# Attention's matmuls in a written order on TensorE, and every other instruction placed by the scheduler on its timeline model

## The chip, the cores and the metric

The kernel runs on one core of one Trainium2 chip. The metric is the device time of one execution in microseconds (us): the kernel before takes 2864.3 us (median of 3 runs, 2860.72 to 2870.65). The trace quoted below is of one further execution of the same kernel, which took 2866.75 us; its span, from the first to the last recorded instruction, is 2865.0 us.

## What is computed

One decoder layer for 2048 prompt tokens and 32 sample tokens (8 sequences of 4), model width 1024. Two branches read the same projection of the normed input: an HGRN2 recurrence (4 heads, a 128 by 128 state each) and sliding-window attention (window 128, 8 query heads on 2 key heads, a sink in the softmax). Gates merge them, and a squared-ReLU feed-forward network follows.

```python
h = _rmsnorm(x, n1)
z = h @ w_in                                   # hq, hf, hi, hg, sq, sk, sv, ga, gb
f = lb + (1.0 - lb) * jax.nn.sigmoid(hf)
o_hg, s_new = _hgrn_recurrence(heads(hq), heads(jnp.log(f)), heads(1.0 - f), heads(hi), s0, 64)
o_hg = _rmsnorm(o_hg, hg_norm_w)
y_a = (o_hg * jax.nn.silu(hg)) @ w_up_a
q, k = _rotary(sq, pos), _rotary(sk, pos)
o_b = _swa_prompt(q, k, v, sinks)              # or _swa_sample for the sample tokens
y_b = o_b @ w_up_b
x = x + (jax.nn.sigmoid(ga) * y_a + jax.nn.sigmoid(gb) * y_b) @ w_o
h2 = _rmsnorm(x, n2)
x = x + jnp.square(jax.nn.relu(h2 @ w_ff1)) @ w_ff2
```

## The kernel before, in words

Five engines work from queues of their own, each in order: PE (TensorE: matmuls, transposes), DVE (VectorE), ACT (ScalarE), POOL (GpSimd) and SP (DMA issues). Every large product is made in three matmuls, because each float32 operand is split into a high and a low part in the type fp32r: high by high, high by low, low by high. In the trace these are the three lines L162, L163, L164 (`gemm_T`), L188 to L190 (`gemm_NK`) or L262 to L264 (`prod`). Scores, transposes and the HGRN products work in plain float32, in matmuls of 128 columns.

The tokens stand in four blocks of 512, b0 to b3; b3 also carries the 32 sample tokens. Blocks b0 and b1 make the half "sb 0", b2 and b3 "sb 1". For sb 0 the in-projection is made block by block; for sb 1 a stage z makes most of it first by Strassen's scheme into memory (tiles fB_z, fC_z, fD_z are its PSUM sums, zS and zA its operands), and b2 and b3 load their parts back. Each block then runs through:

- the remaining projections (hi: tile ps_hib, 96 matmuls of 512 columns in four banks);
- `rotary_T`, which rotates a chunk's queries and keys on POOL (L896 to L899), transposes them on PE (qT, kT) and copies them out on ACT; then `swa_scores` and `swa_values` for the four chunks c0 to c3 of 128 tokens (sp: scores, pT: transposed probabilities, po: values). For b3 the attention of the sample tokens stands ahead of that (sps, pTs, po_s);
- the columns hf of the projection (ps_hfb, four times 24 matmuls), then the HGRN levels (`hgrn_levels`, tiles lv L747 and lx L781) with the columns hg between them;
- per head group the chain o, u, on, kn, oT (L1085 to L1132): PE sums o, ACT squares it, POOL raises it to a power (ors, L195 and L197), DVE scales (on, L1092), PE transposes; u updates the state. For b3 the sample tokens' recurrence follows (o_smp and us, L1141 to L1163), for which SP loads one state per head (L1149);
- the gates b and a (tiles gbb, ybb, gab, yab) and the output projection wob.

After both halves the feed-forward stages f0 and f1 (Strassen again, tiles fB_f, fC_f, fD_f) and f2 (tile f) run. In the Strassen stages seven products share a few PSUM banks; the running sum of a bank is copied out by ACT (L325) or DVE (L327) before the next product adds to it ("snapshot"), and that matmul waits for the copy. `ff_sums` (L578) makes the operand sums of the first feed-forward half: SP loads h2 (L587), four DVE operations sum (L598 to L601), POOL's queue issues the four stores of dS (L603). This is placed beside block 2.

PSUM has the rings mm, tp, hg and sw of two banks each, handed out in program order. What runs when on each engine is decided by the tile framework's scheduler, by priorities that follow the program's order. Only places where the program itself interleaves (a hook between weight groups, hg columns at the rounds 2, 3, 4 and 6 of the levels) are set by hand.

## Time and profile before

| | before |
|---|---|
| three timed runs, us | 2870.65, 2860.72, 2864.3 |
| the profiled execution, us | 2866.75 |
| its span, us | 2865.0 |
| PE busy, us | 2776.3 (97% of the span) |
| DVE, ACT, POOL busy, us | 1786.9, 1113.8, 493.9 |
| mean granted clock of PE | 0.992 |
| instructions in the trace | 50058 |

An engine's busy time counts the time in which at least one of its instructions ran. PE's busy time is no measure of its pace, since matmuls overlap and a matmul at half the clock is busy twice as long; so three things are read for PE: where it idles and for whom, at which clock it runs (a column of the table by stretches), and how far apart the starts of its matmuls lie.

### The profile page before, as it was taken

The page shows a single profiled execution, that of the slowest core. Times are in us where ns is not written, and L with a number is a line of the kernel's source. Part 1 is how long each engine was busy: PE and PEld are TensorE (multiplying, and loading weights), DVE is VectorE, ACT ScalarE, POOL GpSimd, SP SyncE. Part 2 cuts the span into 40 slices and gives each one's busy share as a digit, 9 for nine tenths or more (in the row PEclk, how much of TensorE's full clock was granted, in tenths as well). Part 3 has the DMA queues.
Part 4 walks back from the last instruction along what each step waited for, and adds up shares of the span by engine and source line. Part 5 has one row for each costly group of instructions (what it writes and reads, how often), then busy time and mean ns, then how long its engine had stood idle before and what let it go on. Part 6 is the DMA issues. An engine that isn't in the chain of part 4 may idle for free.

```text
span 2865.0 us, 50058 instructions
## 1 busy us (share of the span) xinstructions
PE 2776.3 (97%) x20053; PEld 2421.9 (85%) x20053; DVE 1786.9 (62%) x2889; ACT 1113.8 (39%) x2070; POOL 493.9 (17%) x782
## 2 busy tenths in 40 slices
PE   8999999999999998999999999999998999999998
PEld 7778877788799966777888888877888999999998
DVE  5585755745765367535766777766567776664546
ACT  4542344423444343234424333434343333343342
POOL 1100211102310112330122221120003343320001
PEclk9999999999999999999999999999999999999999
DMA  5237662277743425642346544697556444485553
GB/s 189 62 91 250 199 200 59 79 252 245 242 142 98 153 61 185 203 139 84 99 154 203 172 155 140 222 318 251 191 192 219 151 145 156 139 294 180 186 186 123
DMA packets 344481, 487.60 MB, mean 170 GB/s; under 512 B 23432, under 2 KB 220824, under 8 KB 344248
## 3 DMA queue, kind: packets, MB, share of 16 engines
q1 hardware_dynamic: 289112, 329.10, 36.5%
q0 software_dynamic: 42880, 140.22, 13.4%
q10 hardware_dynamic: 12256, 15.08, 1.5%
q8 instruction: 157, 2.57, 0.4%
q14 instruction: 76, 0.62, 0.1%
HBM read 353.64 MB, written 130.68 MB: 169 GB/s over the span
## 4 chain that ended last, share of the span: by engine, by line
PE 78%; DMA 7%; issue 5%; DVE 5%; ACT 2%; POOL 2%; SPq 0%; POOLq 0%; ACTq 0%; DVEq 0%
PE f L1494 6%; PE f L1493 6%; PE f L1495 6%; PE fB_f L262 4%; PE fB_f L264 4%; PE fB_f L263 4%; PE fD_f L262 2%; PE fD_f L264 2%; PE fD_f L263 2%; PE fB_z L262 1%; PE fB_z L264 1%; PE fB_z L263 1%; PE wob L1302 1%; PE wob L1303 1%; PE wob L1301 1%
## 5 line engine op out<-in xcount | busy, mean ns | idle before, releaser
L1493 PE MATMUL f<-f2S,hw2T 128*128 128x264 f32 (+1 forms) x576 | 184.3, 320 | 2.8 <-ACT hw2T L148 2.8
L1495 PE MATMUL f<-f2S,lw2T 128*128 128x264 f32 (+1 forms) x576 | 184.3, 320 | 1.1 <-DVE lw2T L149 1.1
L1494 PE MATMUL f<-f2S,hw2T 128*128 128x264 f32 (+1 forms) x576 | 184.0, 319 | 0.0
L262 PE MATMUL fB_f<-S,w1T_f 128*128 128x264 f32 (+1 forms) x384 | 123.0, 321 | 3.2 <-ACT c_f L325 2.2
L1493 PE MATMUL f<-f2A,h_w2B 128*128 128x264 f32 (+1 forms) x384 | 122.4, 319 | 0.0
L1494 PE MATMUL f<-f2A,h_w2B 128*128 128x264 f32 (+1 forms) x384 | 122.3, 318 | 0.0
L1495 PE MATMUL f<-f2A,l_w2B 128*128 128x264 f32 (+1 forms) x384 | 122.3, 318 | 0.0
L263 PE MATMUL fB_f<-S,w1T_f 128*128 128x264 f32 (+1 forms) x384 | 122.3, 319 | 0.0
L264 PE MATMUL fB_f<-S,w1T_f 128*128 128x264 f32 (+1 forms) x384 | 121.9, 319 | 0.0
L149 DVE TENSOR_TENSOR lw2T<-lw2T,hw2T 128x1024 fp32r<-128x1024 f32 x64 | 78.2, 1223 | 69.3 <-ACT hw2T L148 68.6
L148 ACT CAST hw2T<-lw2T 128x1024 fp32r<-128x1024 f32 x64 | 67.2, 1050 | 134.5 <-DMA lw2T<-w_T 134.5
L1493 PEld LDWEIGHTS f<-f2S,hw2T 128*128 128x128 f32 x576 | 108.8, 189 | 11.2 <-ACT hw2T L148 3.7
L1495 PEld LDWEIGHTS f<-f2S,lw2T 128*128 128x128 f32 x576 | 108.4, 188 | 9.5 <-DVE lw2T L149 1.9
L1494 PEld LDWEIGHTS f<-f2S,hw2T 128*128 128x128 f32 x576 | 108.7, 189 | 7.5
L1303 PE MATMUL wob<-m_b,l_wob 128*128 128x512 f32 (+2 forms) x320 | 112.0, 350 | 2.8 <-DVE l_wob L255 2.8
L1301 PE MATMUL wob<-m_b,h_wob 128*128 128x512 f32 (+2 forms) x320 | 112.2, 351 | 0.5 <-ACT m_b L254 0.5
L1302 PE MATMUL wob<-m_b,h_wob 128*128 128x512 f32 (+2 forms) x320 | 112.1, 350 | 0.3 <-DVE m_b L255 0.2
L149 DVE TENSOR_TENSOR f2S<-f2S 128x1024 fp32r<-128x1024 f32 (+1 forms) x64 | 79.1, 1240 | 43.8 <-ACT f2S L148 43.4
L254 ACT CAST w1T_f<-w1r_f 128x512 fp32r<-128x512 f32 x128 | 77.3, 620 | 71.4 <-DVE w1r_f L298 32.4
L255 DVE TENSOR_TENSOR w1T_f<-w1r_f,w1T_f 128x512 fp32r<-128x512 f32 x128 | 87.1, 687 | 27.0 <-ACT w1T_f L254 26.7
L1420 POOL DMA_DIRECT2D u_A<-c_f x106 | 57.5, 543 | 235.3 <-DVE c_f L1404 223.7
L1420 POOL DMA_DIRECT2D u_S<-s_f x144 | 77.9, 542 | 110.9 <-DVE s_f L1415 89.3
(839 smaller groups left out, 9375.7 us busy)
## 6 DMA issues: line engine op xcount, KB each, us to landing
w1r_f<-w_ff SPq DMA_DIRECT2D x64, 512.0 KB
lw2T<-w_T SPq DMA_DIRECT2D x64, 512.0 KB
rw2B<-w_ff SPq DMA_DIRECT2D x48, 512.0 KB
f2S<-u_S SPq DMA_DIRECT2D x32, 528.0 KB
ws<-w_ff SPq DMA_DIRECT2D x32, 512.0 KB
r_wob<-w_o SPq DMA_DIRECT2D x32, 512.0 KB
f2S<-u_S SPq DMA_DIRECT2D x32, 512.0 KB
u_S<-s_f POOLq DMA_DIRECT2D x96, 132.0 KB, 2.2
```

The source lines that it names most:

```text
L149: nc.vector.tensor_tensor(lo, F(lo), F(hi), ALU.subtract)
L255: nc.vector.tensor_tensor(dl, src, F(dh), ALU.subtract)
L262: nc.tensor.matmul(ps, wh, ah, start=(first and k == 0), stop=False, skip_group_check=not first)
L263: nc.tensor.matmul(ps, wh, al, start=False, stop=False, skip_group_check=not first)
L264: nc.tensor.matmul(ps, wl, ah, start=False, stop=(last and k == 3), skip_group_check=not first)
L1301: nc.tensor.matmul(p, wh, ah, start=(k == 0), stop=False)
L1302: nc.tensor.matmul(p, wh, al, start=False, stop=False)
L1303: nc.tensor.matmul(p, wl, ah, start=False, stop=(k == KD - 1))
L1420: nc.gpsimd.dma_start(us[o][u.n // 4][u.n % 4 * P:(u.n % 4 + 1) * P, u.t0:u.t0 + u.ln], y_)
L1493: nc.tensor.matmul(ps, wh, ah, start=first, stop=False, skip_group_check=cont)
L1494: nc.tensor.matmul(ps, wh, al, start=False, stop=False, skip_group_check=cont)
L1495: nc.tensor.matmul(ps, wl, ah, start=False, stop=lastk, skip_group_check=cont)
```

## The change

The change has two parts.

First, a region in which the written order is PE's order. `tc.manual_schedule(engines={PE})` is entered ahead of the sample attention and left behind all attention and the columns hf and the first hg column; the other engines stay free. Inside, attention is cut into steps: T (rotary and transposes), S (scores), P (transposed probabilities), V (values), and a list names the order, with so many matmuls of the columns hf and hg (generator `col_steps`) between them. The second group of scores takes its bank from the ring hg instead of sw, po from tp instead of sw, po_s from tp instead of hg. The products hi of block b3 move ahead of the prompt's attention, with the steps of the sample attention between their weight groups. Evacuations of hg column 0 are held back until round 2 of the levels.

Second, `TileContext(nc, schedule_with_timeline_sim=True)`: all other instructions, in all stages and on all engines, are placed by the scheduler on a timeline model of the machine instead of by priority.

Line numbers move with the added lines: `prod` and the helpers keep theirs, L902 becomes L919, L1149 becomes L1200, and so on.

The instructions themselves are the same in number and kind; only their order, the banks named above and the waits differ.

```diff
+        def col_steps(c0, h, name, fn, held=None):
+            wh, wl = unit_rows(w_in, 0, KD, c0 + h * P, P, name)
+            for (t0, n) in segs:
+                ps = mm_ps(f"ps_{name}_{t0}")
+                for k in range(KD):
...
+                        nc.tensor.matmul(ps[:, 0:n], wt[:, k, :], r, start=(k == 0 and i == 0), stop=(k == KD - 1 and i == 2))
...
+                                if fn is None:
+                                    held.append((ps[:, o:o + ln], kind, d0, ln, h))
...
+                        yield
...
+        pe_order = tc.manual_schedule(engines={mybir.EngineType.PE})
+        pe_order.__enter__()
...
-            po = psum("hg", 2, "po_s")
...
+            def smp_values():
+                po = tp_ps("po_s")
...
+        if zs and odd:
+            nc.gpsimd.dma_start(qW, kmaj(zd[sb], 0, HH, z0 + ns, bt))
+            smp_at = {0: lambda: [smp_scores(kv) for kv in range(NKV)], 1: lambda: [smp_turn(kv) for kv in range(NKV)], 2: smp_values} if smp else {}
+            colN512(C_HI, f"hi{B}", ev_v, lambda i, ul: smp_at[i]() if i in smp_at else None)
...
-                sps = [sw_ps(f"sp_{N}_{gp}_{kv}").rearrange("p (j h k) -> p j h k", j=2, h=2) for kv in range(NKV)]
+                sps = [(sw_ps, hg_ps)[gp](f"sp_{N}_{gp}_{kv}").rearrange("p (j h k) -> p j h k", j=2, h=2) for kv in range(NKV)]
...
-            po = sw_ps(f"po_{N}")
+            po = tp_ps(f"po_{B}c{c}")
...
-        for c in range(ncb + 1):
-            if c < ncb:
-                swa_scores(c)
-            if c > 0:
-                swa_values(c - 1)
+        hg_held = []
+        fills = [col_steps(C_HF, h, f"hf{B}{h}", ev_f) for h in range(HH)] + [col_steps(C_HG, 0, f"hg{B}0", None, hg_held)]
...
+        T_, S_, P_, V_ = swa_turn, swa_scores, swa_probs, swa_values
+        for f, c in ((T_, 0), (fill, 6), (S_, 0), (T_, 1), (fill, 12), (S_, 1), (T_, 2), (fill, 30), (P_, 0), (fill, 10), (V_, 0), (S_, 2), (T_, 3), (fill, 10), (P_, 1),
+                     (fill, 10), (V_, 1), (S_, 3), (fill, 10), (P_, 2), (fill, 8), (V_, 2), (fill, 16), (P_, 3), (fill, 8), (V_, 3)):
+            f(c * len(segs) if f is fill else c)
+        fill(1000)
+        pe_order.__exit__(None, None, None)
...
-        for h in range(HH):
-            colT(C_HF, h, f"hf{B}{h}", ev_f)
...
+                for a in hg_held:
+                    ev_g(*a)
+                hg_held = []
+                if h:
+                    colT(C_HG, h, f"hg{B}{h}", ev_g)
...
-    with tile.TileContext(nc) as tc:
+    with tile.TileContext(nc, schedule_with_timeline_sim=True) as tc:
```

Three places of PE's queue show what moves. The first is the start of block 2's attention. Before, on PE, behind the last Strassen products of z come the 96 matmuls of ps_hib, of which the last four are shown, then the first transposes qT and kT of chunk c0, then columns hf:

```order
L190 MATMUL ps_hib_3_9403<-h_hib_9496,hT_6258 128x512
L188 MATMUL ps_hib_3_9403<-h_hib_9496,hT_6258 128x512
L189 MATMUL ps_hib_3_9403<-l_hib_9497,hT_6258 128x512
L190 MATMUL ps_hib_3_9403<-h_hib_9496,hT_6258 128x512
L902 MATMUL qT_b2c_9534<-ident,qkv_b_9394 128x128 x4
L905 MATMUL kT_b2c_9540<-ident,qkv_b_9394 128x128
L162 MATMUL ps_hfb_0_9877<-hT_6257,h_hfb_9873 128x512
L163 MATMUL ps_hfb_0_9877<-hT_6257,h_hfb_9873 128x512
L164 MATMUL ps_hfb_0_9877<-hT_6257,l_hfb_9874 128x512
L902 MATMUL qT_b2c_9596<-ident,qkv_b_9394 128x128
```

Now, in the same place of PE's queue, with the last three of twelve products fD_z of stage z ahead:

```order
L262 MATMUL fD_z_9_264_9333<-zS_1_6963,w1B_z_9_9136 128x264
L263 MATMUL fD_z_9_264_9333<-zS_1_6963,w1B_z_9_9136 128x264
L264 MATMUL fD_z_9_264_9333<-zS_1_6963,w1B_z_9_9136 128x264
L189 MATMUL ps_hib_3_9409<-l_hib_9503,hT_6264 128x512
L190 MATMUL ps_hib_3_9409<-h_hib_9502,hT_6264 128x512
L919 MATMUL qT_b2c_9542<-ident,qkv_b_9400 128x128 x4
L922 MATMUL kT_b2c_9548<-ident,qkv_b_9400 128x128
L677 MATMUL ps_hfb_0_9558<-hT_6263,h_hfb_9554 128x512 x2
L677 MATMUL ps_hfb_0_9558<-hT_6263,l_hfb_9555 128x512
L677 MATMUL ps_hfb_0_9558<-hT_6263,h_hfb_9554 128x512 x2
L677 MATMUL ps_hfb_0_9558<-hT_6263,l_hfb_9555 128x512
L1041 MATMUL sp_b2c_0_0_9565<-kt_b2c_9550,SV_b_9399 128x128
```

Behind the last product of z now stand only two matmuls of ps_hib ahead of qT; the other 94 have moved in between the products of z.

The second place is the recurrence of the sample tokens in b3 (o_smp reads a loaded state S, us writes the update). Before, on PE, groups of ybb (twelve matmuls each; the first two rows here are the end of one, the last three the start of the next) stand between the steps:

```order
L163 MATMUL ybb_0_14030<-ob_b_11883,h_ubb_13998 128x288
L164 MATMUL ybb_0_14030<-ob_b_11883,l_ubb_13999 128x288
L1161 MATMUL us_0_13873<-vb_13870,kn_smp 128x512
L1161 MATMUL us_1_13876<-vb_13870,kn_smp 128x512
L1152 MATMUL o_smp<-S_2_13859,qb 32x128 x8
L1150 MATMUL o_smp<-vS,W_b_11552 32x128
L162 MATMUL ybb_288_14079<-ob_b_11883,h_ubb_14061 128x256
L163 MATMUL ybb_288_14079<-ob_b_11883,h_ubb_14061 128x256
L164 MATMUL ybb_288_14079<-ob_b_11883,l_ubb_14062 128x256
```

Now, in the same place:

```order
L1212 MATMUL us_0_13843<-vb_13840,kn_smp 128x512
L1212 MATMUL us_1_13846<-vb_13840,kn_smp 128x512
L1203 MATMUL o_smp<-S_1_13850,qb 32x128 x4
L1201 MATMUL o_smp<-vS,W_b_11561 32x128
L1151 MATMUL oT_b3o_13927<-ident,on_b3o_13806 128x128 x4
L1212 MATMUL us_0_13864<-vb_13861,kn_smp 128x512
L1212 MATMUL us_1_13867<-vb_13861,kn_smp 128x512
L1203 MATMUL o_smp<-S_2_13871,qb 32x128 x8
L1212 MATMUL us_0_13885<-vb_13882,kn_smp 128x512
L1212 MATMUL us_1_13888<-vb_13882,kn_smp 128x512
L1201 MATMUL o_smp<-vS,W_b_11561 32x128
```

The steps now follow each other directly; the groups of ybb stand behind the last one or before the chain.

The third place is in stage f1, where the product with S (T3) and the one with A (T4) share a bank (fB_f). Before, on PE, six matmuls into other banks (one of fB_f's second bank and five of fD_f) lie between the two:

```order
L262 MATMUL fB_f_1_0_19686<-S_1_19469,w1T_f_1_20183 128x264
L263 MATMUL fB_f_1_0_19686<-S_1_19469,w1T_f_1_20183 128x264
L264 MATMUL fB_f_1_0_19686<-S_1_19469,w1T_f_1_20183 128x264
L264 MATMUL fB_f_1_264_19728<-S_1_19313,w1T_f_1_20177 128x264
L262 MATMUL fD_f_1_264_20332<-S_1_19389,w1T_f_1_20180 128x264
L263 MATMUL fD_f_1_264_20332<-S_1_19389,w1T_f_1_20180 128x264
L264 MATMUL fD_f_1_264_20332<-S_1_19389,w1T_f_1_20180 128x264
L262 MATMUL fD_f_1_264_20332<-S_1_19389,w1T_f_1_20180 128x264
L263 MATMUL fD_f_1_264_20332<-S_1_19389,w1T_f_1_20180 128x264
L262 MATMUL fB_f_1_0_19686<-A_1_19551,w1T_f_1_20229 128x264
L263 MATMUL fB_f_1_0_19686<-A_1_19551,w1T_f_1_20229 128x264
```

Now, for a neighbouring block of the same stage:

```order
L262 MATMUL fB_f_0_264_19647<-S_1_19481,w1T_f_0_20037 128x264
L263 MATMUL fB_f_0_264_19647<-S_1_19481,w1T_f_0_20037 128x264
L264 MATMUL fB_f_0_264_19647<-S_1_19481,w1T_f_0_20037 128x264
L262 MATMUL fB_f_0_264_19647<-A_1_19563,w1T_f_0_20040 128x264
L263 MATMUL fB_f_0_264_19647<-A_1_19563,w1T_f_0_20040 128x264
L264 MATMUL fB_f_0_264_19647<-A_1_19563,w1T_f_0_20040 128x264
L262 MATMUL fB_f_0_264_19647<-A_1_19563,w1T_f_0_20040 128x264
```

The product with A follows the product with S in the same bank, with nothing between them.

More of the change, by code (lines that the diff above doesn't have):

```diff
@@ L942, in tile_hybrid_step, with smp_scores @@
             nc.sync.dma_start(nvs[0].rearrange("b w v d -> w b (v d)")[0:W - DS], vc.rearrange("p (b e) -> p b e", b=DB)[DS:W])
-            for kv in range(NKV):
+            s_smp, pT_smp = [], []
+            def smp_scores(kv):
                 pr = slice(kv * HD, (kv + 1) * HD)
-                sp = sw_ps(f"sps{kv}")
+                sp = (sw_ps, tp_ps)[kv](f"sps{kv}")
                 for b in range(DB):
@@ L964, in tile_hybrid_step, with smp_turn @@
                 nc.vector.tensor_scalar(s, s, sm, None, ALU.mult)
+            def smp_turn(kv):
+                s = s_smp[kv]
                 tp = tp_ps(f"pTs{kv}")
```

76 lines of the change are left out of this document (46 added, 30 removed).

## The prediction

> **What bounds the kernel now.** I read the page's first two parts first: is there an engine that is busy nearly all the time, and at which clock?
>
> ```profile
> PE 2776.3 (97%) x20053; PEld 2421.9 (85%) x20053; DVE 1786.9 (62%) x2889; ACT 1113.8 (39%) x2070; POOL 493.9 (17%) x782
> ```
>
> PE is the bound. The span is 2865.0 us, so only 2865.0 - 2776.3 = 88.7 us of it are idle on PE. The same instructions stay, so a new order can gain three things: part of those 88.7 us, part of what a lowered clock costs, and part of what the spacing of the matmuls costs. For the first I read PE's waits by what ended them (us in total, times, longest).
>
> ```profile
> PE ps_hib L188 <- ACT h_hib L254: 9.3, 1, 9.3
> PE u_b2o L1127 <- DVE on_b2o L1092: 6.2, 1, 6.2
> PE fB_f L262 <- ACT c_f L325: 5.2, 3, 3.0
> PE n_fb L213 <- DVE p_f L340: 5.2, 1, 5.2
> PE fB_f L262 <- DVE y L1500: 4.2, 1, 4.2
> PE fC_z L262 <- DVE p_z L340: 3.0, 1, 3.0
> PE fB_f L262 <- DVE c_f L327: 2.9, 3, 1.3
> PE lv_b2g L747 <- issue: 2.8, 1, 2.8
> PE yab L162 <- DVE ga_b L1188: 2.7, 2, 2.2
> PE ps_hfb L162 <- ACT W_b L679: 2.1, 1, 2.1
> PE fB_z L262 <- ACT stg L809: 2.1, 1, 2.1
> PE po_s L972 <- ACT pTs L970: 2.0, 1, 2.0
> PE lv_b3g L747 <- issue: 2.0, 1, 2.0
> PE o_b2o L1121 <- ACT W_b L784: 1.8, 1, 1.8
> PE u_b3o L1127 <- DVE on_b3o L1092: 1.4, 1, 1.4
> PE u_b1o L1127 <- ACT junk L202: 1.3, 1, 1.3
> PE lv_b0g L747 <- issue: 1.3, 1, 1.3
> PE sp_b1c L1004 <- DVE W_b L1012: 0.9, 1, 0.9
> ```
>
> The reader is to see that the idle time is in many small pieces. 9.3 us are the kernel's start, waiting for the first weights; a change of order does nothing there. Attention, which the written order is about, owns few rows: ps_hfb, po_s, sp_b1c. Block 2's HGRN part owns the most.
>
> For the clock I read the table of stretches (its columns: stretch, length, busy of PE, PEld, DVE, ACT, POOL, granted clock, DMA share, GB/s).
>
> ```profile
> 90.00:170.00 80.00, 77.75 (x953) 53.22 (x955) 57.89 (x119) 34.84 (x111) 5.10 (x11) 1.00 0.22 66
> 1085.00:1135.00 50.00, 42.02 (x716) 34.88 (x717) 33.46 (x67) 21.59 (x56) 10.28 (x18) 0.90 0.53 170
> 1135.00:1200.00 65.00, 61.83 (x277) 50.09 (x276) 41.33 (x57) 18.97 (x31) 18.85 (x21) 0.97 0.59 200
> 1350.00:1360.00 10.00, 7.83 (x49) 7.28 (x48) 4.54 (x9) 3.79 (x6) 0.00 (x0) 0.83 1.14 315
> 1560.00:1570.00 10.00, 6.96 (x24) 5.66 (x25) 7.99 (x13) 3.92 (x5) 3.80 (x2) 0.66 0.22 83
> 1920.00:1950.00 30.00, 26.11 (x105) 20.24 (x104) 23.18 (x28) 13.76 (x14) 5.42 (x10) 0.94 0.95 341
> ```
>
> The first row is most of block 0's attention: PE is busy 97% of it at the full clock, so waits of attention are worth little. The others show what a stall costs beyond itself: the 2.1-us wait of ps_hfb lies in 1350 to 1360 and drops the clock there to 0.83, 10 x 0.17 = 1.7 us; the 5.2-us wait of n_fb drops 1560 to 1570 to 0.66, 3.4 us.
>
> **The change part by part: gains.** *Attention's waits* (ps_hfb 2.1, po_s 2.0, sp_b1c 0.9) go: in the written order po_s comes behind a group of ps_hib and the columns hf of b3 no longer follow the small score products at once. With the clock at ps_hfb: 5.0 + 1.7 = **6.7 us**. The cover is the hf and hg columns; where they run out, the next late thing is the softmax on DVE, which that row has at 72% busy.
>
> *Changes of type.* A short stretch of block 0's attention shows the spacing (start, duration, then the instruction):
>
> ```profile
> 94.93 0.40 PE L163 MATMUL ps_hfb<-hT,h_hfb 128*128 128x512 f32 x1
> 95.26 1.16 PE L1004 MATMUL sp_b0c<-kt_b0c,SV_b 64*128 64x128 f32 x16
> 96.35 0.50 PE L164 MATMUL ps_hfb<-hT,l_hfb 128*128 128x512 f32 x1
> 96.68 0.39 PE L162 MATMUL ps_hfb<-hT,h_hfb 128*128 128x512 f32 x1
> 96.91 0.39 PE L163 MATMUL ps_hfb<-hT,h_hfb 128*128 128x512 f32 x1
> ```
>
> From one column matmul to the next it is 96.91 - 96.68 = 0.23 us; from a column matmul to a score 95.26 - 94.93 = 0.33; from the first column matmul behind the scores to the second 96.68 - 96.35 = 0.33. Going to plain float32 and back costs 0.10 + 0.10 = 0.20 us, which no wait shows. Counting PE's order of both programs, such round trips fall by about 50 (entries 124 to 75, returns 96 to 46): 50 x 0.20 = **10 us**.
>
> *HGRN of b0, b1, b3.* The waits lv_b3g 2.0, u_b3o 1.4, u_b1o 1.3, lv_b0g 1.3 make **6.0 us**. In the new order groups of ybb, gbb or hg stand between those steps. Bounds: 0 to 6.0; I take all, since each is shorter than one group of 24 such matmuls (24 x 0.23 = 5.5 us).
>
> *HGRN of block 2.* The waits u_b2o 6.2, lv_b2g 2.8, o_b2o 1.8 and yab's longest 2.2 make 13.0 us; the clock adds 50 x 0.10 + 65 x 0.03 = 7.0; together 20.0. In the new order the levels are filled, but no ybb group is left for the last two links of the chain o, on, oT, and POOL's queue has the stores dS of two more rounds of `ff_sums` ahead of the first ors. Bounds 0 to 20.0; I take half, **10 us**, because the levels keep their filler and the chain loses it.
>
> *Stage z.* fC_z 3.0 and fB_z 2.1 are covered by ps_hib, which now lies among z's products: **5 us**.
>
> **Losses.** *The start of block 2's attention.* The three rows: the loads that follow z's last product, and the first and last rotation step of chunk c0 and PE's first transpose.
>
> ```profile
> 990.39 2.13 POOL L884 DMA_DIRECT2D qkv_b<-zqk  x4 [2.87 <-PE fB_z L264]
> 996.38 1.35 POOL L896 TENSOR_TENSOR r_b2c<-qkv_b,rot 128x80 f32<-128x80 f32 x1 [3.86 <-ACT c_z L837]
> 999.62 0.54 POOL L899 TENSOR_TENSOR qkv_b<-qkv_b,r_b2c 128x160 f32<-128x160 f32 x1
> 1012.98 0.60 PE L902 MATMUL qT_b2c<-ident,qkv_b 128*128 128x128 f32 x4
> ```
>
> The chain takes from z's last product (about 990.1) to 999.62 + 0.54 = 1000.16, so 10.1 us, and PE comes to qT only at 1012.98: 96 matmuls of ps_hib (96 x 0.23 = 22 us) hid it. Now twelve products of 264 columns (0.12 us each, by the rows of the next part) and two of 512 stand there: 12 x 0.12 + 2 x 0.23 = 1.9 us. PE waits 10.1 - 1.9 = 8.2 us, and the clock falls as at n_fb, 3.4 us: **11.6 us**. SP's and POOL's loads cannot start earlier, because the memory is z's operand slot (the first row's releaser is fB_z).
>
> [...]
>
> *The sample tokens' recurrence.* SP's issue of the load of the last state and the o_smp that used it:
>
> ```profile
> 1445.74 0.38 SPq L1149 DMA_DIRECT2D S<-state_hgrn  x1
> 1449.98 1.91 PE L1152 MATMUL o_smp<-S,qb 128*32 128x128 f32 x16 [0.16 <-DMA S<-state_hgrn]
> ```
>
> The load of the last state takes 1449.98 - 1445.74 = 4.2 us and ends last. A group of ybb of 12 matmuls (0.12 to 0.13 us each, 1.5 to 1.6 us) stands before in each of the intervals of the last two loads, and in neither now: 2 x 1.6 = 3.2 us, and once a drop of the clock of 1.7: **4.9 us**. Bounds 3.2 and 2 x 4.2 = 8.4; I stay near the low one, since o_smp and us remain.
>
> *Same-bank products in f0 and f1.* A place in z shows what a snapshot takes when little lies between:
>
> ```profile
> 825.15 0.28 PE L264 MATMUL fB_z<-zS,w1T_z 128*128 128x264 f32 x1
> 825.27 0.28 PE L262 MATMUL fB_z<-zS,w1T_z 128*128 128x264 f32 x1
> 825.47 0.38 ACT L325 COPY c_z<-fB_z 128x264 f32<-128x264 f32 x1 [2.53 <-PE fB_z L264]
> 825.90 0.39 PE L262 MATMUL fB_z<-zA,w1T_z 128*128 128x264 f32 x1
> ```
>
> The bank's last matmul starts at 825.15, the copy ends at 825.85, the next product starts at 825.90: 0.75 us against a spacing of 825.27 - 825.15 = 0.12. So a place without cover costs 0.63 us. Counted in the new order, 19 waits in f0 and f1 have no cover and 8 have two matmuls (0.63 - 2 x 0.12 = 0.4): 19 x 0.63 + 8 x 0.4 = 15.2 us; before, none. Against that, the longer waits there (fB_f 5.2 + 4.2 + 2.9 = 12.3) come from backlogs on ACT and DVE, and waits whose cover is 1 to 2.5 us fall from about 255 to 170: I take half, 6.2 us off. Net **9.0 us**, bounds 2.9 and 15.2.
>
> *At nothing:* the start (9.3), n_fb (it stands behind the same 48 products), f2 and the tail, whose orders hardly differ.
>
> **The sum.** Gains 6.7 + 10 + 6.0 + 10 + 5 = 37.7; losses 11.6 + 4.9 + 9.0 = 25.5; net 12.2. The profiled execution took 2866.75, which gives 2854.5; it lies 2.45 us above the median of the runs, so on the median's footing 2864.3 - 12.2 = **2852 us**.
>
> **The rivals.** What a measurement of this kernel can tell from no change is about 0.3%, 8.6 us: 2855.7 to 2872.9.
>
> *The whole order gets deeper and the backlogs go.* The small stalls of the Strassen stages end with ACT or DVE working off what came at once. If all 12.3 us of fB_f go instead of half (6.2 more), the clock at 1920 to 1950 with them (30 x 0.06 = 1.8), and block 2's HGRN gives 20.0 instead of 10: 18 more, 2834. For it speaks that DVE is only 62% busy; against it the counted places without cover.
>
> *POOL's queue holds block 2's chain.* The stores of rounds three and four wait for loads and four DVE operations each; on_b2o waits for ors behind them. A round has a load of some 4.2 us (as above) and a store beside 2.7 us of DVE work. One full round on the path costs about 4.2 + 2.7 + 2.1 (the four POOL issues of the row at 990.39 take 2.13) = 9.0, with the clock 12.4: 2864, and both rounds 2877. It decides if the fourth round's first DVE operation comes later than o_b2o is ready.
>
> *The clock falls with the small stalls* (the slower side). A 30-us stretch with a few stalls of f already runs at 0.94. If 15 or more of the 27 same-bank places drop the clock by 1.7 us each, 25 us come on top and the kernel is slower than 2873; if 22 do, 2889. For it: 2.1 us of idling were enough at ps_hfb. Against it: 0.63 us alone is a third of that.
>
> [...]
>
> That the change does not move the work is excluded by the orders.
>
> **How the numbers follow.** Forecast 0.42 (2838 to 2866 by its bounds: 0.27 faster, 0.13 same, 0.02 slower); deeper order 0.24, faster; POOL's queue 0.16 (0.06 same, 0.10 slower); clock 0.18, slower. Faster 0.51, same 0.19, slower 0.30. The range leaves out a third of the first rival's lower tail (0.08) and the clock's upper part (0.10): 2822 to 2888.
>
> **What would show it.** PE waiting about 8 us for qT_b2c behind POOL's rotation, at a clock near 0.66 over the next 10 us. No row ps_hfb, po_s or sp_b1c. Waits of fB_f by c_f many (over 20) and short, instead of six of 8.1 us. o_smp waiting for the load of S for over 1.5 us twice. The forecast is wrong if PE's idle time without start falls under 50 us (deeper order), if u_b2o or oT_b2o waits over 9 us behind ors (POOL), or if the clock in 2080 to 2330 is below 0.95.

## The result and the profile after

The changed kernel takes 2894.83 us (median of 4 runs, 2885.62 to 2908.49), the kernel before beside it 2865.31 us (4 runs, 2860.72 to 2870.65). The ratio is 1.0104 (95% interval 1.0065 to 1.0144): slower by 29.5 us, where 12 us faster were forecast and the range ended at 2888. The profiled execution took 2890.7 us at a mean granted clock of 0.983 (before 0.992).

The first lines of the page after:

```profile
span 2888.9 us, 50057 instructions
PE 2757.2 (95%) x20053; PEld 2423.4 (84%) x20053; DVE 1785.9 (62%) x2889; ACT 1102.0 (38%) x2070; POOL 489.5 (17%) x782
```

Read against before, these two lines say two opposite things. PE's idle time is 2888.9 - 2757.2 = 131.7 us instead of 88.7: 43.0 us more waiting. But PE's busy time fell by 2776.3 - 2757.2 = 19.1 us, and that at a lower clock: (1 - 0.983) x 2889 = 49 us are lost to the clock after, (1 - 0.992) x 2865 = 23 before. Part of that lies in PE's own waits, where a low clock costs nothing; counted over PE's busy time in the stretches of lowered clock alone, it is 31 us after and 17 before. So the matmuls themselves stand some 19 + 14 = 33 us closer together at equal clock (an estimate from these figures), and 43 us of waits and 14 us of clock take more than that away: 43.0 - 19.1 = 23.9 us, the difference of the spans.

PE's waits after, by what ended them (us in total, times, longest; left out here are the kernel's start with 7.6 us and some rows of 4.5 us and less):

```profile
PE fB_f L262 <- ACT c_f L325: 13.3, 19, 3.3
PE u_b2o L1178 <- ACT kn_b2o L1160: 10.2, 1, 10.2
PE fB_f L262 <- DVE c_f L327: 9.3, 9, 2.7
PE fD_f L262 <- ACT S L148: 6.2, 1, 6.2
PE qT_b2c L919 <- POOL qkv_b L916: 5.5, 1, 5.5
PE fD_f L262 <- DVE c_f L370: 5.4, 4, 2.8
PE o_smp L1203 <- DMA S<-state_hgrn: 4.5, 1, 4.5
PE fC_z L262 <- DVE p_z L340: 4.2, 1, 4.2
PE fD_f L262 <- DVE c_f L357: 3.4, 1, 3.4
PE sp_b2c L1041 <- ACT kt_b2c L924: 3.3, 1, 3.3
PE po_b1c L1088 <- DVE pc_b1c L1079: 2.8, 2, 1.5
PE o_b3o L1172 <- ACT W_b L801: 2.2, 1, 2.2
PE po_b3c L1088 <- DVE pc_b3c L1079: 1.9, 2, 1.4
PE po_b0c L1088 <- DVE pc_b0c L1079: 1.7, 1, 1.7
```

The feed-forward's rows fB_f and fD_f make 13.3 + 9.3 + 6.2 + 5.4 + 3.4 = 37.6 us; before they were 12.3 for fB_f and 1.4 for fD_f. Most of the other new waiting is at block 2: u_b2o 10.2 instead of 6.2, qT_b2c 5.5 and sp_b2c 3.3, which were not there; o_smp adds some 4 and the three rows po 6.4.

To see where the time went I cut the traces at the same matmuls (the last of each stage; for z block 2's first transpose, for f1 the first matmul of f2's second half) and took the distance between the cuts. The columns with numbers are experiments, told below; each column is one profiled execution.

| stretch, us | before | after | 1 | 2 | 7 | 8 | 9 | 10 | 12 |
|---|---|---|---|---|---|---|---|---|---|
| b0, to the end of wob | 372.1 | 366.5 | 375.0 | 365.5 | 364.8 | 364.8 | 366.8 | 366.8 | 364.7 |
| b1 | 369.9 | 362.8 | 380.1 | 361.0 | 361.4 | 362.2 | 363.5 | 361.2 | 361.3 |
| z, to block 2's first transpose | 271.0 | 279.2 | 289.1 | 269.9 | 278.5 | 268.9 | 275.7 | 279.9 | 279.5 |
| b2 | 214.4 | 222.2 | 204.3 | 219.1 | 223.0 | 210.2 | 225.8 | 225.3 | 222.6 |
| b3 | 317.5 | 311.8 | 338.2 | 321.6 | 319.9 | 317.6 | 317.8 | 318.0 | 322.2 |
| f0 and f2's first half | 627.2 | 629.8 | 634.2 | 628.4 | 626.6 | 631.5 | 633.2 | 643.7 | 632.7 |
| f1 | 348.6 | 371.6 | 371.5 | 347.8 | 369.0 | 346.0 | 345.3 | 362.4 | 375.3 |
| f2's second half | 331.6 | 330.0 | 330.7 | 331.8 | 335.4 | 330.8 | 331.7 | 334.3 | 330.0 |

The blocks b0 and b1 gain 12.7 us, z and b2 lose 16.0, and f1 alone loses 23.0. Stretches with the same order of PE differ between executions: b3 is 311.8 in this one and 317.8 to 319.9 in the experiments 7, 9 and 10, which have exactly its order there, and b0, b1, z and b2 differ by up to some 4 us among these. So b3's gain of 5.7 is not read, nor is a difference under about 5 us elsewhere. The loss in f1 is far outside that. From f0 on all queues stand in one and the same order in the changed kernel and in experiments 1 and 12, and f1 takes 371.5 to 375.3; they stand in another, again the same for all three, in the kernel before and in experiments 2 and 8, and f1 takes 346.0 to 348.6.

**The mechanism, in three places.** The first is block 2's HGRN chain. ACT's queue and PE's matmul that waits for it (start, duration, instruction, in brackets the idle time before it and what ended that), with the issue of the load on SP ahead:

```profile
1139.86 10.40 SPq L138 DMA_DIRECT2D r_wob<-w_o  x1
1143.01 0.19 ACT L202 ACTIVATION_READ_ACCUMULATOR junk<-o_b2o 128x1 f32 x1
1154.77 1.04 ACT L254 CAST h_wob<-r_wob 128x1024 fp32r<-128x1024 f32 x1 [11.57 <-DMA r_wob<-w_o]
1155.72 0.58 ACT L1160 COPY kn_b2o<-kn_b2o 128x512 f32<-128x512 f32 x1
1156.35 2.08 PE L1178 MATMUL u_b2o<-SV_b,kn_b2o 128*128 128x128 f32 x8 [10.22 <-ACT kn_b2o L1160]
```

kn_b2o is a copy of 0.58 us. It stands in ACT's queue behind a cast of the output projection's weights, and that cast waits 11.57 us for its load. Nothing is wrong with the chain; its next link merely queues behind something that isn't due for a long while. The load's issue stands on SP for 10.40 us, where those just before it on that queue took 0.35 to 0.38; what held it the profile does not tell.

The second place is the load of one of the Strassen operands ahead of f1, after:

```profile
2216.78 1.45 POOL L608 DMA_DIRECT2D S<-dS  x2
2223.51 1.07 ACT L148 CAST S<-S 128x1056 fp32r<-128x1056 f32 x1 [6.41 <-DMA S<-dS]
2224.64 0.59 PE L262 MATMUL fD_f<-S,w1B_f 128*128 128x264 f32 x1 [6.20 <-ACT S L148]
```

and the same load before:

```profile
2213.04 1.45 POOL L608 DMA_DIRECT2D S<-dS  x2
2217.79 1.07 ACT L148 CAST S<-S 128x1056 fp32r<-128x1056 f32 x1 [0.63 <-DMA S<-dS]
```

The issue comes 3.74 us later on POOL, from there to the cast it takes 6.73 us instead of 4.75, ACT idles 6.41 us for it instead of 0.63, and PE stands 6.2 us behind it.

The third is DVE in f1:

```profile
2248.34 0.69 DVE L296 TENSOR_TENSOR w1r_f<-w1r_f,w1r_f 128x512 f32<-128x512 f32 x1 [2.24 <-DMA w1r_f<-w_ff]
2248.95 0.42 DVE L357 TENSOR_TENSOR c_f<-fD_f,c_f 128x264 f32<-128x264 f32 x1
2249.43 0.59 PE L262 MATMUL fD_f<-S,w1B_f 128*128 128x264 f32 x1 [3.41 <-DVE c_f L357]
```

The snapshot c_f, for which PE waits, stands behind a weight sum that waits 2.24 us for weights. Not every long wait has a load in it. Some 17 us later DVE works without a pause through at least nine sums and casts for other products, and the snapshot that PE waits for stands behind them:

```profile
2265.75 0.42 DVE L327 TENSOR_TENSOR c_f<-fB_f,p_f 128x264 f32<-128x264 f32 x1
2266.23 0.49 PE L262 MATMUL fB_f<-S,w1T_f 128*128 128x264 f32 x1 [2.67 <-DVE c_f L327]
```

Over the whole program ACT idles 846.5 us for a DMA's landing (before 694.7) and DVE 74.8 us (before 50.4). That is idling on engines that are no bound, and it costs only where something PE needs stands behind it.

What it does to the clock, and to f1 as a whole (2172.40 to 2544.00), shows in the table of stretches after (columns as in the prediction):

```profile
1000.00:1100.00 100.00, 87.40 (x1014) 65.60 (x1013) 63.92 (x126) 40.63 (x121) 19.35 (x35) 0.91 0.42 130
2214.00:2240.00 26.00, 17.07 (x95) 15.25 (x94) 10.65 (x21) 6.26 (x12) 6.45 (x12) 0.74 0.44 141
2240.00:2340.00 100.00, 86.74 (x664) 83.95 (x663) 68.61 (x151) 28.35 (x60) 33.22 (x62) 0.97 0.38 127
2249.00:2253.00 4.00, 3.57 (x17) 3.57 (x18) 1.77 (x6) 0.09 (x1) 1.07 (x2) 0.57 0.20 69
2266.00:2270.00 4.00, 3.15 (x14) 2.88 (x15) 0.96 (x3) 0.00 (x0) 1.95 (x4) 0.57 0.74 260
2270.00:2340.00 70.00, 64.37 (x512) 62.70 (x512) 51.03 (x114) 21.58 (x45) 24.11 (x45) 1.00 0.35 118
2172.40:2544.00 371.60, 342.24 (x2673) 333.79 (x2672) 261.28 (x531) 129.57 (x272) 122.65 (x226) 0.97 0.46 153
```

and before (f1 there from 2172.10 to 2520.70):

```profile
1000.00:1100.00 100.00, 96.98 (x1117) 68.96 (x1115) 64.48 (x127) 41.26 (x122) 14.97 (x26) 0.98 0.29 84
2214.00:2240.00 26.00, 22.68 (x168) 21.90 (x167) 19.44 (x39) 9.96 (x21) 8.63 (x16) 0.93 0.52 164
2172.10:2520.70 348.60, 334.75 (x2685) 331.62 (x2685) 258.37 (x536) 130.66 (x271) 126.06 (x231) 0.99 0.48 159
```

Behind the 6.2-us wait the clock is 0.74 over 26 us, behind the two waits at block 2's start 0.91 over 100. In the stretch 2240 to 2340 PE idles 13 us in many pieces and the clock stays at 0.97; what is lost there lies right behind the waits of 3.41 and 2.67 us shown above (0.57 over 4 us each time), and the clock is 1.00 from 2270 to 2340, over six waits of 0.5 to 0.7 us and one of 2.4. So in this stretch the clock is lost behind the few long waits and not behind the short ones. What it costs shows in the starts: behind the wait of 2.67 us matmuls of 264 columns start 0.22 us apart (2266.74 - 2266.52), against 0.12 at the full clock (825.27 - 825.15, before). Of f1's 23 us PE's idle time makes (371.60 - 342.24) - (348.60 - 334.75) = 15.5, and part of the rest is the clock (0.97 against 0.99).

### The profile page after: what moved, and what is told of

Its sections match the earlier page's. It is cut to its first block, busy times and chain, and to the rows that moved or that the text cites. A ratio compares the mean times of both kernels' runs of the same rounds, so it can differ in the third digit from the quotient of the medians.

```text
span 2888.9 us, 50057 instructions
## 1 busy us (share of the span) xinstructions
PE 2757.2 (95%) x20053; PEld 2423.4 (84%) x20053; DVE 1785.9 (62%) x2889; ACT 1102.0 (38%) x2070; POOL 489.5 (17%) x782
## 3 DMA queue, kind: packets, MB, share of 16 engines
q0 software_dynamic: 42880, 140.22, 13.5%
## 4 chain that ended last, share of the span: by engine, by line
PE 75%; DMA 10%; DVE 7%; issue 4%; ACT 3%; POOL 1%; SPq 0%; ACTq 0%; POOLq 0%; DVEq 0%
PE f L1545 7%; PE f L1544 7%; PE f L1546 7%; PE fB_f L262 4%; PE fB_f L264 4%; PE fB_f L263 4%; PE fD_f L262 2%; PE fD_f L264 2%; PE fD_f L263 2%; PE wob L1353 2%; PE wob L1354 2%; PE wob L1352 2%; PE fB_z L262 1%; PE fB_z L264 1%; DMA r_wob<-w_o 1%
## 5 line engine op out<-in xcount | busy, mean ns | idle before, releaser
L1471 POOL DMA_DIRECT2D u_A<-c_f x106 | 57.3, 541 | 311.7 <-DVE c_f L1455 307.3
L254 ACT CAST w1B_f<-w1r_f 128x512 fp32r<-128x512 f32 x96 | 58.6, 621 | 126.6 <-DMA w1r_f<-w_ff 56.1
L255 DVE TENSOR_TENSOR l_w2B<-rw2B,h_w2B 128x1024 fp32r<-128x1024 f32 x48 | 58.7, 1224 | 67.9 <-ACT h_w2B L254 61.3
```

Source lines behind the costliest of these rows:

```text
L254: nc.scalar.copy(dh, src)
```

## The experiments

Each was run beside the kernel before on the same chip; a difference between two experiments is best read from their ratios to it. My first theory was that the change's two parts have opposite signs: the written order wins, and the timeline model, which places the queues of ACT, DVE, POOL and SP too, loses. The rival was that PE's new order is what loses, by places without cover.

### 1 and 2: each part alone

The model alone, on the kernel before:

```diff
-    with tile.TileContext(nc) as tc:
+    with tile.TileContext(nc, schedule_with_timeline_sim=True) as tc:
```

> The kernel before with nothing changed but the scheduler's timeline model; attention is written and interleaved as before. Theory A (the model's placement loses, the written order of attention gains): slower than the changed kernel by what attention gained there, some 10 to 20 us, so 2905 to 2915 us, with f1 still about 20 us longer than before. Theory B (the written order of attention loses, in its waits for po and at block 2's start; the model is harmless): within 5 us of before, 2860 to 2870 us. Theory C (the many short stalls lower the clock): a mean clock near 0.98, and time lost in proportion to it.

Measured: 2940.49 us against 2869.72, ratio 1.0233 (1.0212 to 1.0253).

The written order alone, on the changed kernel:

```diff
-    with tile.TileContext(nc, schedule_with_timeline_sim=True) as tc:
+    with tile.TileContext(nc) as tc:
```

> The changed kernel without the timeline model: attention's matmuls in the written order, all else placed by priority as before. Theory A: faster than before by the terms of attention in the prediction, 6.7 us of waits and some of the 10 us of type changes: 2848 to 2858 us, clock near 0.992. Theory B: slower than before, 2875 us or more. Theory C: the clock of before, and with it the time of before within 5 us.

Measured: 2856.21 us, ratio 0.9950 (0.9934 to 0.9966).

What follows: the model alone costs 70.8 us, the written order alone wins 13.5, and both together lose 29.5. Theory A has both signs and experiment 2's time; for the model alone its 2905 to 2915 us was 25 us too low. The effects don't add (70.8 - 13.5 = 57.3): with the model on, the written order is worth 70.8 - 29.5 = 41 us. The likely reason is that it takes attention's matmuls out of the model's hands, since b0, b1 and b3 are where the model alone is longer than the changed kernel (8.5, 17.3 and 26.4 us). In the table of stretches f1 is 371.5 with the model alone and 347.8 with the order alone: the loss in f1 belongs to the model.

### 3 and 4: PE's order exchanged between the two schedules

In both, PE's matmuls are tied one behind the other, by dependencies of the class NoSync, in a list taken from the other kernel (the list is left out). In experiment 3 the model places everything but PE, which runs in the order of the kernel before; in experiment 4 priorities place everything but PE, which runs in the model's order.

```diff
+    def pe_in_order():
...
+        by = {i.name: i for i in nc.cur_bb.bb.instructions}
+        for p, q in zip(order, order[1:]):
+            tc.add_manual_dep(by[f"I-{q}"], f"I-{p}", mybir.DependencyInfo(mybir.DependencyClass.NoSync, mybir.DependencyReason.DATA), reason="pe order")
```

> The timeline model as in the run with the model alone, but PE's 17671 matmuls and transposes are chained in the order that the kernel before has; the model places only the other engines' instructions. Theory A1 (the queues of ACT, DVE, POOL and SP are placed badly: loads and casts ahead of what PE needs): still slower than before by 15 us or more. Theory A2 (PE's own order is what loses: products that follow each other in one bank, too little ahead of block 2's rotation): within 6 us of before, 2860 to 2871 us.

Measured: 2945.53 us, ratio 1.0266 (1.0247 to 1.0285).

> The kernel before, placed by priority, but PE's matmuls and transposes chained in the order that the timeline model gave in the run with the model alone; the other engines are placed by priority around it. Theory A1: near before, 2860 to 2872 us. Theory A2: as slow as the run with the model alone, 2895 us or more. If both lose in part, each of the two runs lies between.

Measured: 2960.5 us, ratio 1.0315 (1.0295 to 1.0335).

What follows: neither half is the culprit by itself. PE's good order with the model's other queues is as slow as the model alone, and PE's model order with the good queues is slower still; f1 is 364.1 and 361.0 in them, 15.5 and 12.4 us over before. I read this as a mismatch: an order of PE and the orders of the engines that feed it fit each other, and a mixture of two schedules over the whole program costs. So these two don't separate the theories, and the later ones exchange queues in one stage only.

### 5: block 2's weight casts behind its chain

On the changed kernel; the casts of block 2's output weights are placed behind the last ACT instruction of its HGRN chain:

```diff
+            last_sq = next(i for i in reversed(nc.cur_bb.bb.instructions) if i.engine == mybir.EngineType.Activation)
...
-            uo = [unit_rows(w_o, 4 * kh, 4, n * P, 2 * P, f"wo{B}{n}{kh}") for kh in range(2)]
+            with tc.issue_after(last_sq) if bi == 2 else ExitStack():
+                uo = [unit_rows(w_o, 4 * kh, 4, n * P, 2 * P, f"wo{B}{n}{kh}") for kh in range(2)]
```

> The changed kernel, with ACT's casts of block 2's output weights (h_wob) issued behind the last squares of the chain o, u, on of that block; in the changed kernel two of them stand ahead of the copy kn_b2o, and one waits 11.6 us for its load. Theory D (a cast that waits for a late load at the head of ACT's queue holds PE): u_b2o's wait of 10.2 us goes, and with it the low clock behind it, 10 to 14 us less than the changed kernel, 2881 to 2885 us against its 2895. Rival E (the chain itself is late, through POOL's powers and DVE): the wait only moves to u_b2o, oT or yab behind DVE, and under 4 us are won.

Measured: 2896.86 us, ratio 1.0094 (1.0070 to 1.0118). PE's waits in it that bear on block 2:

```profile
PE yab L162 <- ACT oa_b L254: 8.0, 1, 8.0
PE oT_b2o L1151 <- DVE on_b2o L1143: 3.3, 1, 3.3
```

and ACT's queue, with the matmul behind it:

```profile
1156.67 1.04 ACT L254 CAST h_wob<-r_wob 128x1024 fp32r<-128x1024 f32 x1 [9.03 <-DMA r_wob<-w_o]
1157.62 2.17 ACT L254 CAST oa_b<-W_b 128x512 fp32r<-128x512 f32 x4
1158.28 2.07 PE L162 MATMUL yab<-oa_b,h_uab 128*128 128x512 f32 x4 [8.01 <-ACT oa_b L254]
```

What follows: the wait of 10.2 us at u_b2o is gone, so its cause was that cast. But 8.0 us came back at yab. The same cast, which still waits for the same late load (9.03 us), now stands ahead of oa_b, so the edit moved the obstacle by one link of the chain and did not remove it. The wait moved as rival E said, but behind ACT and not behind DVE. b2 went from 222.2 to 217.2 in the trace, hardly more than its scatter, and the time of the whole did not change.

### 6: the products hi of block 2 inside the written order

On the changed kernel; the 96 matmuls that had hidden block 2's first rotation move behind the start of the written region, as b3's already do:

```diff
-            colN512(C_HI, f"hi{B}", ev_v)
...
-        if zs and odd:
-            nc.gpsimd.dma_start(qW, kmaj(zd[sb], 0, HH, z0 + ns, bt))
+        if zs:
+            if odd:
+                nc.gpsimd.dma_start(qW, kmaj(zd[sb], 0, HH, z0 + ns, bt))
```

> The changed kernel, with the 96 products hi of block 2 inside the region of written order, ahead of the first transposes; 36 of them (8 us) now stand behind z's last product instead of 2. Theory F (block 2's start loses because its cover went into z): the waits for qT_b2c (5.5) and sp_b2c (3.3) and the low clock there go, 9 to 14 us less than the changed kernel: 2881 to 2886 us. Rival G (the products were worth as much inside z as they are behind it): z gets longer by as much, and the time stays within 4 us of the changed kernel's.

Measured: 2896.54 us, ratio 1.0098 (1.0079 to 1.0117). The stretch at block 2's start:

```profile
1000.00:1100.00 100.00, 94.11 (x1140) 70.46 (x1139) 73.40 (x139) 47.12 (x131) 23.25 (x39) 0.98 0.51 156
```

What follows: the wait for qT_b2c is gone and the clock is back at 0.98, as before the change; z and b2 are 3.5 and 1.5 us shorter in the trace, no more than the same stretches differ between executions. The whole is not measurably faster, as rival G had it, though z did not get longer. So no gain is shown at the place whose wait and clock the prediction had priced at 11.6 us; with the changed kernel's interval (1.0065 to 1.0144) the times alone do not exclude one of that size.

### 7, 9 and 10: f's queues exchanged, by groups of engines

On the changed kernel, from f0 on, some engines' instructions are tied in the order that experiment 2 gives them, and the model places the rest. The tie is that of experiment 3, for several queues:

```diff
+    def queues_in_order():
...
+            for p, q in zip(order, order[1:]):
+                tc.add_manual_dep(by[f"I-{q}"], f"I-{p}", mybir.DependencyInfo(mybir.DependencyClass.NoSync, mybir.DependencyReason.DATA), reason="queue order")
```

What is placed by the model is placed anew around the tied instructions: of the 1349 instructions that DVE has from f0 on in experiment 7, those that stand in the changed kernel's sequence are 664, and those in the sequence of experiment 2 are 1038 (by a comparison of the traces). So these runs test the model's placing of an engine, and not the changed kernel's very queue.

Experiment 7 ties PE's products alone.

> The changed kernel, with PE's matmuls of f0, f1 and f2 chained in the order that they have without the timeline model; the other engines stay on the model. f1 takes 348.6 us in the kernel before and 371.6 in the changed one, 364.1 with PE's order of before and the model for the rest, 361.0 the other way round. If PE's order is what loses (products that follow each other in a bank): f1 near 350 and 20 us less in all, 2875 us. If the other engines' order is: f1 near 364 and 7 us less. If both, as the two swaps suggest: 356 to 364, 8 to 15 us less.

Measured: 2896.46 us, ratio 1.0098 (1.0075 to 1.0121). PE's waits for the running sums in it:

```profile
PE fB_f L262 <- DVE c_f L327: 14.0, 8, 3.2
PE fB_f L262 <- ACT c_f L325: 6.2, 5, 2.1
PE fD_f L262 <- ACT S L148: 6.1, 1, 6.1
```

This is the most telling list of the study. With the good order on PE the places where fB_f waits fall from 19 + 9 = 28 to 5 + 8 = 13, and yet the two rows still make 20.2 us instead of 22.6, because each wait is longer: the snapshot comes when DVE and ACT get to it. f1 is 369.0, and the time of the whole is the changed kernel's; even the smallest gain that was expected, 7 us, does not show.

Experiment 9 ties PE, ACT and DVE; POOL and SP stay with the model.

> The changed kernel, with PE, ACT and DVE chained, from f0 on, in the order that they have without the timeline model; POOL and SP stay on the model. With PE alone chained, f1 kept 369 of its 372 us. Theory J (the order of ACT's and DVE's casts, sums and snapshots loses in f1): f1 falls to about 350 us and the kernel to 2875 us. Theory K (the order of the load and store issues on POOL and SP loses): f1 stays above 362 us.

Measured: 2872.08 us (10 runs), ratio 1.0013 (0.9997 to 1.0029). Its f1:

```profile
2182.70:2528.00 345.30, 333.72 (x2685) 330.61 (x2685) 255.35 (x533) 128.43 (x268) 125.56 (x231) 0.99 0.49 161
```

Experiment 10 ties PE, POOL and SP; ACT and DVE stay with the model.

> The changed kernel, with PE, POOL and SP chained, from f0 on, in the order that they have without the timeline model; ACT and DVE stay on the model. Theory J: f1 stays above 362 us. Theory K: f1 falls to about 350 us and the kernel to 2875 us, and the wait of fD_f for the load and cast of S (6 us) goes.

Measured: 2897.18 us, ratio 1.0101 (1.0078 to 1.0124). Its f1:

```profile
2194.90:2557.40 362.50, 335.75 (x2686) 331.43 (x2686) 260.07 (x538) 132.13 (x272) 125.35 (x231) 0.98 0.48 157
```

What follows: with ACT's and DVE's order put back beside PE's, the loss against the kernel before falls from 29.5 to 2.8 us, f1 is 345.3, and PE idles 11.6 us in it (345.30 - 333.72) against 13.9 before the change and 29.4 after it. With POOL's and SP's put back instead, the issue of the loads among them, nothing measurable goes from the whole, f1 is 362.4, PE idles 26.8 us in it, and its wait for the cast of S stays (7.1 us, one time). So, with PE's order the same in both, f1's loss is made by the order of casts, weight sums and snapshots on ACT and DVE. Experiment 9 alone would not exclude POOL, whose queue the model there puts nearly in experiment 2's order by itself (423 of 433 instructions in sequence); experiment 10, which has POOL's and SP's queues in that order (432 of 433 and 339 of 339) and keeps most of the loss, does. That POOL's order alone made the cast of S late, which the rows of the second place suggest, is refuted. ACT's and DVE's order with the model's own order of PE was not run, so whether PE's order matters beside theirs stays open.

### 8 and 12: the gate's first column left at the levels

On experiment 2 (no model), and then on the changed kernel:

```diff
-        fills = [col_steps(C_HF, h, f"hf{B}{h}", ev_f) for h in range(HH)] + [col_steps(C_HG, 0, f"hg{B}0", None, hg_held)]
+        fills = [col_steps(C_HF, h, f"hf{B}{h}", ev_f) for h in range(HH)]
...
-                if h:
-                    colT(C_HG, h, f"hg{B}{h}", ev_g)
+                colT(C_HG, h, f"hg{B}{h}", ev_g)
```

> The written order without the timeline model, with hg column 0 left at its old place among the HGRN levels, so that attention has only the columns hf between its steps. Theory H (taking hg column 0 into attention robs the levels of what lay between them): the waits of lv in blocks 2 and 3 (14 us with the low clock left out) fall to the 5 us of before, and the time is 8 to 15 us under the written order alone (2856 us): 2841 to 2848 us. Rival I (attention needs those 24 matmuls more): waits for po and pT take their place, and the time is 2855 us or more.

Measured: 2844.57 us against 2868.06, ratio 0.9914 (0.9898 to 0.9930). This is the fastest version here, 23.5 us better than the kernel before. Against experiment 2 b2 is 8.9 us shorter (PE idles 17.5 us in it instead of 23.5), and the mean granted clock of the whole is 0.990 instead of 0.984. Theory H gave the time. That the fourth column fills the levels is only in part what the waits show: lv_b2g falls from 5.8 to 4.7 us, u_b2o's 4.8 go, and o_b2o rises from 2.9 to 5.4. The 5.2 us that PE waited at lv_b3g in experiment 2 go too, but that wait was ended by nothing that the profile shows, and 4.8 us of the same kind stand in the middle of a group of hg here.

> The changed kernel, timeline model on, with hg column 0 left at its old place among the HGRN levels. Without the model this part is worth 12 us. Theory N (the column is missing at the levels whoever places the rest): 8 to 15 us under the changed kernel, 2880 to 2887 us. Rival O (the model fills the levels with ybb and gbb groups anyway): within 5 us of the changed kernel, 2890 to 2900 us.

Measured: 2906.33 us against 2869.3, ratio 1.0130 (1.0115 to 1.0146). PE's waits in it for the chain of block 2 and block 3:

```profile
PE o_b2o L1171 <- DVE state L1182: 9.9, 2, 6.8
PE o_b3o L1171 <- ACT W_b L801: 8.0, 1, 8.0
```

and what stands on ACT ahead of the copy W_b that o_b3o waits for:

```profile
1412.60 1.04 ACT L254 CAST h_uab<-r_uab 128x1024 fp32r<-128x1024 f32 x1 [7.23 <-DMA r_uab<-w_up_a]
```

What follows: by the medians the same edit wins 11.6 us without the model and loses 11.5 with it; against the kernel before beside each it is 10 won and 7.5 lost. The gain is clear of the noise. The loss is not: the intervals of experiment 12 and of the changed kernel (1.0065 to 1.0144) overlap. What is shown is that with the model a gain of that size does not come; theory N's 2880 to 2887 us are missed by far, and rival O's 2890 to 2900 us too. The rows o_b2o (2.0 in the changed kernel) and o_b3o (2.2) show where PE waits in that schedule, and for o_b3o the cause is the one of block 2 again: a weight cast that waits 7.23 us for its load stands ahead of the copy. Why the model places the chain so is open.

### 11: the key heads one after the other

On experiment 8; the two key heads' scores, which alternate in the kernel's text, are written one head after the other:

```diff
-                for j in range(2):
-                    g = gp * 2 + j
-                    for w in range(nj):
-                        for kv in range(NKV):
+                for kv in range(NKV):
+                    for j in range(2):
+                        g = gp * 2 + j
+                        for w in range(nj):
```

> The fastest kernel so far (written order, no timeline model, hg column 0 left at the levels; 2844.6 us), with the loops of the scores turned: all four of one key head, then all four of the other, in place of the two heads in turn. Theory L (two score matmuls on the two halves of the array's rows run side by side when they stand next to each other: their starts are 7 ns apart, those of the same half 105): some 240 spacings grow from 7 to 105 ns, 23 us more, 2862 to 2870 us. Rival M (the gain in the scores comes from fewer changes of type): no change, 2841 to 2849 us.

Measured: 2849.94 us, ratio 0.9940 (0.9918 to 0.9962). The scores of a first stretch of block 0 in experiment 8, and the instruction behind them:

```profile
96.59 2.06 PE L1041 MATMUL sp_b0c<-kt_b0c,SV_b 64*128 64x128 f32 x32
98.58 0.66 PE L919 MATMUL qT_b0c<-ident,qkv_b 128*128 128x128 f32 x4
```

and in experiment 11:

```profile
96.89 2.82 PE L1041 MATMUL sp_b0c<-kt_b0c,SV_b 64*128 64x128 f32 x32
99.64 0.65 PE L919 MATMUL qT_b0c<-ident,qkv_b 128*128 128x128 f32 x4
```

32 scores take 98.58 - 96.59 = 1.99 us alternating, 62 ns each, and 99.64 - 96.89 = 2.75 us, 86 ns each, one head after the other. Over all 496 scores the distances of starts add up to 30.9 and 42.4 us: 11.5 us, half of the 23 that I had expected. The medians differ by 5.4 us, but the intervals overlap and the two profiled spans are equal (2845.1), so in the time of the whole it is not separated; theory L's 2862 to 2870 us are excluded, and the median lies 1 us above rival M's range.

## Why the prediction was wrong, point by point

| term | forecast, us | what the runs showed |
|---|---|---|
| attention's waits | -6.7 | the three rows are gone; new waits at po, the three largest 2.8 + 1.9 + 1.7 us, came |
| spacing (changes of type) | -10 | distances from each start to the next, waits left out: scores -17.4, values po -2.6, columns hf -5.8: -25.8 |
| HGRN of b0, b1, b3 | -6.0 | of the four rows 0.4 us at lv_b3g is left; o_b3o has 2.2 |
| HGRN of block 2 | -10 | +4 at u_b2o; b2 as a whole +7.8 |
| stage z | -5 | fB_z gone, fC_z 4.2 instead of 3.0 |
| start of block 2's attention | +11.6 | waits 5.5 + 3.3 and a clock of 0.91 over 100 us came; undoing it wins nothing measurable |
| sample tokens' recurrence | +4.9 | 4.5, in one wait |
| f0 and f1 | +9.0 | f0 with f2's first half +2.6, f1 +23.0 |

**Right.** These places: the wait for qT_b2c behind POOL's rotation with the drop of the clock, the wait of o_smp for its state, the disappearance of the three attention rows, the many short waits of fB_f (28 against 27 counted in the order). Written order alone, 13.5 us, came near the forecast's 12.2, though it is another kernel and its terms are others.

**Mis-sized, in favour.** The spacing term was 10 and measured 25.8. I had counted only type changes. What I didn't see is that the written order puts both key heads' scores side by side: the median distance from a score to the next is 7 ns instead of 107. Experiment 11 confirms the direction for the scores, at half the size.

**The step that failed: f0 and f1.** I counted the places without cover in PE's order, priced them at 0.63 us, and then wrote that the longer waits "come from backlogs on ACT and DVE" and took half of them off, because the intervals of cover got longer. The count was near and the price too high (bare snapshots after take 0.47 to 0.53 us, and the eight of them with two matmuls between take 0.23 instead of 0.4). The sign of the second part was wrong: the backlogs grew. Waits for f's sums and operand came to 37.6 us where 15.2 + 6.2 = 21.4 had been reckoned, and the clock, for which this term had nothing, is 0.74 behind the longest of them. Experiment 7 shows that putting PE's order back wins nothing there, experiments 9 and 10 that ACT's and DVE's order makes the loss. Behind it stands an assumption that the prediction never stated: that, POOL's stores at block 2 apart, only PE's order had to be read, and that the other engines would follow it as before. But the change places all engines anew, and in the new queues of ACT and DVE a cast or sum that waits for a late load, or a row of other sums, stands ahead of what PE needs next.

**The same step failed in block 2.** I had PE's fillers and POOL's stores in view, and half a gain. The 10.2 us came from ACT's queue, behind a cast that the prediction doesn't mention. The rival that POOL's queue holds the chain named the right place and the wrong queue. Part of what b2 lost belongs to the written order itself, without the model: leaving hg column 0 at the levels makes b2 8.9 us shorter (experiment 8 against 2), where the prediction had the levels keep their filler.

**The slower rival** gave 2889, near the measured time, by another way, so that is luck. It wanted the clock to fall with the 27 short waits of f; the clock is 1.00 over the short ones (2270 to 2340), 0.57 over 4 us behind the waits of 3.41 and 2.67, and 0.74 where the longest wait is. The prediction's own sign for it, a clock below 0.95 from 2080 to 2330, did not come: it is 0.96. From 2240 to 2340, with 13 us of idling in 100, it is 0.97.

**The range.** The 2838 to 2866 that the prediction calls the forecast's bounds do not follow from its terms: with the low and the high bound of each taken together they give 2834 to 2878. That would still not have reached 2894.83.

**Open.** Why one edit wins 10 us without the model and none with it (experiments 8 and 12), and what of z's 8.2 us is not the wait for qT_b2c and its clock. Experiments 9 and 2 still differ by 16 us, of which the table has 5.8 in z and 6.7 in b2. That the late loads are what makes f1's order of ACT and DVE bad is read from the single waits shown; no run brought a load forward.

## What to carry to other kernels

When a change hands the order of all engines to a scheduler, read the queues of the engines that feed the bound before its own: look in each for an instruction that waits for a load, and for a row of work that isn't yet due, ahead of what the bound needs next. Moving one such instruction a link further only moved the wait here (10.2 us at u_b2o became 8.0 at yab, experiment 5). Run the parts of such a change alone and together, since here they were -13.5, +70.8 and +29.5 us, and an order that is good for one engine was worth nothing with another schedule's queues around it. Here the version to keep is the written order without the timeline model, with hg column 0 left at the levels: 2844.57 us, 0.86% under the kernel before.

## What the hardware showed that I had not expected

Scores that contract over 64 rows run into each other on PE when two that use different halves of the rows follow one another: starts 7 ns apart in the median in the changed kernel, 62 ns a score in the mean in the group of experiment 8, against 86 ns in that of experiment 11, where one half's scores follow each other. Over a whole group of 32 scores the gain is 2.75 / 1.99 = 1.4 times.

In these stretches a long wait was dear for the clock and the short ones were not: one wait of 6.2 us went with a clock of 0.74 over 26 us, while 70 us with six waits of 0.5 to 0.7 us and one of 2.4 kept 1.00. The rows draw no line between the two: the 2.1 us at ps_hfb before the change went with 0.83 over 10 us.
